# Starting the activations' sums twelve steps earlier, in tiles that begin 224 bytes off a multiple of 256

## The chip, the cores and the metric

The kernel runs on one core of one Trainium2 chip. The metric is the device time of one execution in microseconds (us), as the median of several runs. The engines are named as in the profile: PE (TensorE matmul), PEld (its weight loads), DVE (VectorE), ACT (ScalarE), POOL (GpSimd) and SP (SyncE).

## What is computed

The reference is a trunk of two layers on 256 tokens of width 2048, in float32. Layer 0 mixes with an mLSTM and a gated linear recurrence, layer 1 with dilated attention; each mixer ends in an output projection, and each layer ends in a SwiGLU feed-forward block with 5632 hidden columns. The part that matters here is the norm, the feed-forward block and what stands between them:

```python
x = x + mixer(rmsnorm(x, norm)) @ w_out        # the output projection
h = rmsnorm(x, f_norm[l])
x = x + (jax.nn.silu(h @ w1) * (h @ w3)) @ w2  # the feed-forward block
```

## The kernel before, in words

**Steps.** All weights stream through SBUF once. The kernel writes down a list of `steps`; a step is half of one weight tile: two k-blocks of 128 rows by 512 columns. `emit_step` (L340) runs one step: it splits the weights of the steps up to three ahead (`emit_split`, L213) into a high part on ACT (`wh`, L228) and a low part on DVE (`wl`, L229), issues the step's matmuls, and then calls `run_tasks` (L278) once. A float32 product is made of three matmuls: high by high, high by low, low by high. The activations are the stationary operand (PE loads 128x128 of them per matmul), the weights the moving one.

**Tasks.** Everything that isn't a weight product is a Python generator. `run_tasks` advances each urgent one, then up to three (`CONC`) of the queue, by one `yield`. So a task that yields n times is spread over n steps, and the engines' instructions stand in the order in which steps and tasks wrote them. A step may carry a function under `"before"`, which is called when the step begins, for instance to queue a task. Where a step needs something that a task hasn't made yet, `until` (L286) runs tasks until its flag is set.

**The output projection** (`out_proj`, L1184) has four groups of 512 columns and 32 steps; the last 16 are column groups 2 and 3, eight steps each. When a group ends, `norm_evac` (L407) adds it to the residual `xres` on DVE (L414), squares it on ACT (L417), has PE transpose it into PSUM (`nT`, L146) and writes the transposed, gain-scaled activations in two halves to `xT` (L440 on ACT, L441 on DVE). It then sets the flag of that quarter of `xT`.

**The feed-forward block** (`ffn`, L989) has 11 groups of 512 hidden columns. A group is 16 steps: `w1` and `w3` alternate, two steps each, over the four quarters of `xT`. After its `w3` part the group's result is transposed by PE (`hTp`, L146). After groups 0 to 2, 3 to 5, 6 to 8 and 9 to 10 come the steps of `w2`.

**Seven products.** In groups 1 to 10 the `w1` steps of quarters 1 to 3 (`SEVEN`) multiply a 2x2 block matrix with seven instead of eight block products (`seven_products`, L304): 21 matmuls of 256 columns instead of 12 of 512. For this they need sums of the weights' blocks (`weight_sums`, L197, made anew for each weight tile, `ws` and `wf`) and sums of the activations' blocks. The latter are made once per feed-forward block by the task `act_sums` (L1056) and kept in three tiles `sf`, one per quarter, each with two pairs of k-blocks. For each of the six pairs the task makes one sum over `xT` (L1067), four sums and differences (L1071, L1072, L1074, L1075, into `sb`), a high part on ACT (L1077) and a low part on DVE (L1079), with a `yield` behind each of the five stages. It waits for the flag of its quarter of `xT` first. `seven_products` takes four stationary operands of each pair from `sf`, in high and low: 12 of its 21 matmuls load from it.

**Where the sums begin.** The task is queued by the first step of the feed-forward block (L1117). Group 0 doesn't use its result; group 1 needs the first pair in its fifth step and the sixth pair in its fourteenth.

**Tiles.** `sf`, `hT` (the `w2` operand), the residual `xres` and others take slots of one pool with eight buffers (`slot`, L87), each of 2112 floats, that is 8448 bytes or 33 times 256. A tile begins where its slot begins, at a multiple of 256 bytes.

Of the kernel before, what the change touches and what calls it, by code (L numbers as in the profile page):

```python
# [9 lines left out]
F32 = mybir.dt.float32  # L10
F32R = mybir.dt.float32r
# [6 lines left out]
P = 128  # L18
# [50 lines left out]
def trunk_kernel(ctx: ExitStack, tc: tile.TileContext, a, out):  # L69
# [14 lines left out]
    mxp = ctx.enter_context(tc.tile_pool(name="mxp", bufs=2, space=PSUM))  # L84
    ctx.enter_context(tc.manual_schedule())

    def slot(shape, dt=F32, name="s8"):  # L87
        t = s8p.tile([P, SLOT], dt, tag="s8", name=name)
        n = int(np.prod(shape))
        v = t[:, :n]  # L90
        if len(shape) == 1:
            return v
        pat = {2: "p (a b) -> p a b", 3: "p (a b c) -> p a b c", 4: "p (a b c d) -> p a b c d"}[len(shape)]
        return v.rearrange(pat, **dict(zip("abcd"[1:], shape[1:])))
# [6 lines left out]
    def ev(name="ev"):  # L101
        return evp.tile([P, CW], F32, tag="ev", name=name)
# [50 lines left out]
    steps = []  # L153
    x_in = {}

    def load_xT(k0, n):

        i, r = divmod(k0, 8)
        if i not in x_in:
            x_in[i] = slot((8, S), name="xin")  # L160
        SP.dma_start(x_in[i][:, r:r + n, :], a["xT"][:, k0:k0 + n, :])
# [77 lines left out]
    def add_unit(src, ch, kb0, first, last, act, seven=None):  # L239

        items.append(wload(src, len(items)))
        it = len(items) - 1
        for h in range(2):
            steps.append({
                "item": it, "half": h, "last_half": h == 1, "ch": ch, "kb": kb0 + 2 * h, "act": act,
                "first": first and h == 0, "last": last and h == 1, "wide": False, "before": None, "seven": seven,
            })
# [21 lines left out]
    urgent, queue, active = [], [], []  # L269
# [201 lines left out]
    def rg_block(b):  # L471
        def gen(ch):
            if b == 0:
                rg["xc"] = slot((RB, S), name="xc")
            xc = rg["xc"][:, b, :]
            e = ev("xr")
            xp = e[:, :260]
            V.memset(e[:, 0:2], 0.0)
            V.memset(e[:, 258:260], 0.0)
            while "rstd_e" not in flags:  # L480
                yield
            join(ch.acc[0], e[:, 2:258])
            ch.acc = None
            V.tensor_tensor(e[:, 2:258], e[:, 2:258], cur["rB"], op=ALU.mult)
            yield
            w = cpk[:, C_W + 4 * b:C_W + 4 * b + 4]
            A.activation(
                xc, xp[:, 2:258], AF.Identity, bias=cpk[:, C_B + b:C_B + b + 1], scale=w[:, 2:3],
            )
            for j in (0, 1, 3):  # L490
                V.scalar_tensor_tensor(xc, xp[:, j:j + S], w[:, j:j + 1], xc, op0=ALU.mult, op1=ALU.add)
            if b == RB - 1:
                queue.append(rg_scans())
            yield

        return gen

    def rg_scans():
        while "gates" not in flags:
            yield  # L500
        rg["h"] = slot((RB, S), name="rgh")
        wts = [rg_weights(0)]
        for c in range(RB // 2):
            if c + 1 < RB // 2:
                wts.append(rg_weights(c + 1))
            yield from rg_scan(c, wts.pop(0))
# [482 lines left out]
    def ffn(l, gains, nxt):  # L989
# [64 lines left out]
        sf = {}  # L1054

        def act_sums():  # L1056

            for g in SEVEN:
                while f"xT{gains}_{g}" not in flags:
                    yield  # L1060
                two = slot((2, 4, 2, P), F32R, "sf")
                for j, kb in enumerate((4 * g, 4 * g + 2)):
                    f = two[:, j]
                    v = ev("sa")
                    x = xT[:, kb:kb + 2].bitcast(F32)
                    vv = v.rearrange("p (j t) -> p j t", j=2)
                    V.tensor_tensor(vv, x[:, :, 0, :], x[:, :, 1, :], op=ALU.add)  # L1067
                    a11, a21, a12, a22 = (vv[:, j, t * P:(t + 1) * P] for j in range(2) for t in range(2))
                    w = ev("sb").rearrange("p (k t) -> p k t", k=4)
                    yield  # L1070
                    V.tensor_tensor(w[:, 0], a21, a22, op=ALU.add)  # L1071
                    V.tensor_tensor(w[:, 2], a11, a21, op=ALU.subtract)  # L1072
                    yield
                    V.tensor_tensor(w[:, 1], w[:, 0], a11, op=ALU.subtract)  # L1074
                    V.tensor_tensor(w[:, 3], a12, w[:, 1], op=ALU.subtract)  # L1075
                    yield
                    A.copy(f[:, :, 0, :], w)  # L1077
                    yield
                    V.tensor_tensor(f[:, :, 1, :], w, f[:, :, 0, :].bitcast(F32), op=ALU.subtract)  # L1079
                    sf[kb] = f  # L1080
                    flags.add(f"sf{l}_{kb}")
                    yield
# [5 lines left out]
        at_first = len(steps)  # L1088
        for hidx, (c0, c1) in enumerate(UPS):
# [23 lines left out]
            for n, kgs in ((0, range(c0, c1 - 1)), (1, range(c0, c1 - 1)), (0, (c1 - 1,)), (1, (c1 - 1,)),  # L1113
                           (2, range(c0, c1)), (3, range(c0, c1))):
                for kg in kgs:
                    add_unit(a["w2"][l, n][kg], chs[n], 4 * kg, kg == c0, kg == c1 - 1, act_h)
        steps[at_first]["before"] = lambda: queue.append(act_sums())  # L1117
        return ssq


# [78 lines left out]
    steps[first + 8]["before"] = load_x  # L1199

    ffn(0, G_F0, G_O)

    act = act_norm(G_O)
# [3 lines left out]
    out_proj(a["w_o"], G_F1, act_o, "ssq_o1", ((0, 1, 2), (3,)))  # L1207

    ssq = ffn(1, G_F1, -1)

    def load_fg():
# [25 lines left out]
    n = NCD - 1  # L1237
# [104 lines left out]
```

## Time and profile before

| what | value |
|---|---|
| median of 3 runs | 2220.28 us (2219.53 to 2221.06) |
| the profiled execution: its time | 2219.59 us |
| the profiled execution: its span | 2217.8 us |
| mean granted TensorE clock | 0.996 |
| PE busy | 2195.3 us, 11492 matmuls |
| DVE busy | 1588.9 us |
| ACT busy | 1156.3 us |
| DMA | 417.53 MB, mean 188 GB/s |

The span is what the trace covers, from the first to the last instruction; the 1.8 us between it and the execution's own time lie around it. Busy time on PE counts from a matmul's start to its modelled end, and matmuls overlap, so the distance between the starts of two matmuls says more about PE's pace than their durations. In the list of waits an arrow names the instruction that ended a wait; in the timeline the same stands in brackets, with the idle time ahead of the instruction. The granted clock is the share of TensorE's full clock that it was allowed in a stretch.

### The profile page before, as it was taken

How to read it: one execution, taken by the hardware profiler on the slowest of the kernel's cores; microseconds unless marked ns; L12 is line 12 of the kernel's file. 1: busy time of each engine (PE TensorE's matmuls, PEld its weight loads, DVE VectorE, ACT ScalarE, POOL GpSimd, SP SyncE). 2: the span in 40 equal slices, each digit the busy share in tenths (PEclk: the TensorE clock that was granted, in tenths of full speed). 3: DMA queues.
4: the chain of work that ended last, by engine and by line, in shares of the span. 5: the costliest groups of instructions: out<-in, count | busy, mean ns of one | idle time of the engine just before them, and what ended most of it. 6: DMA issues, size and time to landing. Idle time of an engine off the chain costs nothing.

```text
span 2217.8 us, 28894 instructions
## 1 busy us (share of the span) xinstructions
PE 2195.3 (99%) x11492; PEld 1881.5 (85%) x11492; DVE 1588.9 (72%) x2160; ACT 1156.3 (52%) x1555; POOL 22.6 (1%) x37
## 2 busy tenths in 40 slices
PE   9999999999999999999999999999999999999998
PEld 7887888888888888888888888888888888888886
DVE  6877756875787688578666676567867885886686
ACT  6666555544455455445554555455544553554454
POOL 0000000000000000000000000000000000000000
PEclk9999999999999999999999999999999999999999
DMA  7444555555555555555554555455555655555653
GB/s 280 174 143 148 193 201 199 171 190 190 199 181 207 179 201 201 194 197 191 177 191 174 180 185 175 171 182 180 189 190 190 208 190 190 183 203 197 215 192 131
DMA packets 61471, 417.53 MB, mean 188 GB/s; under 512 B 7060, under 2 KB 7956, under 8 KB 12568
## 3 DMA queue, kind: packets, MB, share of 16 engines
q1 hardware_dynamic: 58616, 406.69, 52.9%
q0 software_dynamic: 2288, 8.39, 1.1%
q8 instruction: 90, 1.47, 0.2%
q10 hardware_dynamic: 432, 0.61, 0.1%
q14 instruction: 45, 0.37, 0.0%
HBM read 413.56 MB, written 2.10 MB: 187 GB/s over the span
## 4 chain that ended last, share of the span: by engine, by line
PE 90%; DVE 6%; ACT 2%; issue 1%; DMA 0%; SPq 0%; POOL 0%; POOLq 0%; DVEq 0%; ACTq 0%
PE acc L300 20%; PE acc L301 20%; PE acc L302 20%; PE acc L361 9%; PE acc L362 5%; PE ext L338 2%; PE ext L337 2%; PE ext L336 2%; DVE wl L229 2%; PE acc L338 2%; PE acc L336 2%; PE acc L337 2%; ACT wh L228 1%; PE hTp L146 1%; PE rgp L524 1%
## 5 line engine op out<-in xcount | busy, mean ns | idle before, releaser
L229 DVE TENSOR_TENSOR wl<-raw,wh 128x1024 fp32r<-128x1024 f32 (+1 forms) x770 | 928.7, 1220 | 519.9 <-ACT wh L228 517.1
L228 ACT CAST wh<-raw 128x1024 fp32r<-128x1024 f32 (+1 forms) x770 | 794.0, 1046 | 518.8 <-PE acc L302 376.2
L300 PE MATMUL acc<-wh,xT 128*128 128x512 f32 x1184 | 467.5, 395 | 0.0
L301 PE MATMUL acc<-wl,xT 128*128 128x512 f32 x1184 | 462.9, 391 | 1.0 <-DVE wl L229 1.0
L302 PE MATMUL acc<-wh,xT 128*128 128x512 f32 x1184 | 461.6, 390 | 0.0
L361 PE MATMUL acc<-xT,wh 128*128 128x512 f32 x896 | 321.7, 402 | 0.5 <-ACT v L731 0.5
L300 PE MATMUL acc<-wh,hT 128*128 128x512 f32 x704 | 276.1, 392 | 0.0
L302 PE MATMUL acc<-wh,hT 128*128 128x512 f32 x704 | 274.3, 390 | 0.0
L301 PE MATMUL acc<-wl,hT 128*128 128x512 f32 x704 | 274.1, 389 | 0.1
L302 PEld LDWEIGHTS acc<-wh,xT 128*128 128x128 f32 x1184 | 222.7, 188 | 47.2
L300 PEld LDWEIGHTS acc<-wh,xT 128*128 128x128 f32 x1184 | 223.4, 189 | 45.7 <-issue 1.5
L301 PEld LDWEIGHTS acc<-wl,xT 128*128 128x128 f32 x1184 | 223.1, 188 | 44.9 <-DVE wl L229 2.3
L362 PE MATMUL acc<-xT,wl 128*128 128x256 f32 x896 | 251.2, 280 | 0.2 <-DVE wl L229 0.2
L209 ACT CAST wf<-ws 128x512 fp32r<-128x512 f32 x180 | 111.9, 622 | 201.1 <-DVE ws L202 152.5
L361 PEld LDWEIGHTS acc<-xT,wh 128*128 128x128 f32 x896 | 168.3, 188 | 39.5 <-ACT v L731 0.6
L362 PEld LDWEIGHTS acc<-xT,wl 128*128 128x128 f32 x896 | 169.2, 189 | 1.1 <-DVE wl L229 0.5
L302 PEld LDWEIGHTS acc<-wh,hT 128*128 128x128 f32 x704 | 132.1, 188 | 27.8
L301 PEld LDWEIGHTS acc<-wl,hT 128*128 128x128 f32 x704 | 132.3, 188 | 27.4 <-DVE wl L229 0.5
L300 PEld LDWEIGHTS acc<-wh,hT 128*128 128x128 f32 x704 | 132.2, 188 | 26.8
L210 DVE TENSOR_TENSOR wf<-ws,wf 128x512 fp32r<-128x512 f32 x180 | 113.3, 684 | 0.0
L338 PE MATMUL ext<-wf,sf 128*128 128x256 f32 x240 | 68.7, 286 | 4.6 <-DVE sf L1079 4.6
L336 PE MATMUL ext<-wf,sf 128*128 128x256 f32 x240 | 68.3, 285 | 3.6 <-ACT sf L1077 3.6
(278 smaller groups left out, 2731.8 us busy)
## 6 DMA issues: line engine op xcount, KB each, us to landing
raw<-in_w SPq DMA_DIRECT2D x264, 1024.0 KB, 4.9
raw<-in_w_aqk SPq DMA_DIRECT2D x32, 1024.0 KB, 4.9
raw<-in_w_out SPq DMA_DIRECT2D x16, 1024.0 KB, 4.9
raw<-in_w_av SPq DMA_DIRECT2D x16, 1024.0 KB, 4.9
raw<-in_w_o SPq DMA_DIRECT2D x16, 1024.0 KB, 4.9
raw<-in_w_xr SPq DMA_DIRECT2D x8, 1024.0 KB, 6.8
raw<-in_w_qk SPq DMA_DIRECT2D x8, 1024.0 KB, 4.9
raw<-in_w_og SPq DMA_DIRECT2D x8, 1024.0 KB, 4.8
```

The costliest lines, as they stand in the source:

```text
L209: A.copy(f[:, 0], t)
L210: V.tensor_tensor(f[:, 1], t, f[:, 0].bitcast(F32), op=ALU.subtract)
L228: A.copy(hi[:, k], raw[:, k])
L229: V.tensor_tensor(lo[:, k], raw[:, k], hi[:, k].bitcast(F32), op=ALU.subtract)
L300: PE.matmul(acc, xh, hi[:, j, :], start=f, stop=False)
L301: PE.matmul(acc, xh, lo[:, j, :], start=False, stop=False)
L302: PE.matmul(acc, xl, hi[:, j, :], start=False, stop=e)
L336: PE.matmul(o, xh, wh, start=new, stop=False)
L337: PE.matmul(o, xh, wl, start=False, stop=False)
L338: PE.matmul(o, xl, wh, start=False, stop=end)
L361: PE.matmul(acc, wh[:, j, :], x2.rearrange("p a b -> p (a b)"), start=f, stop=False)
L362: PE.matmul(acc[:, :S], wl[:, j, :], x2[:, 0, :], start=False, stop=e)
```

## The change

Two things change. The task `act_sums` is queued by the step that lies twelve before the feed-forward block's first, in the fifth of the eight steps of the output projection's column group 2. And `slot` gets an argument `off`, with which the `sf` tiles begin 56 floats, 224 bytes, behind the start of their slot (they have 2048 floats, so they still fit).

```diff
-    def slot(shape, dt=F32, name="s8"):
+    def slot(shape, dt=F32, name="s8", off=0):
         t = s8p.tile([P, SLOT], dt, tag="s8", name=name)
         n = int(np.prod(shape))
-        v = t[:, :n]
+        v = t[:, off:off + n]
...
-                two = slot((2, 4, 2, P), F32R, "sf")
+                two = slot((2, 4, 2, P), F32R, "sf", off=56)
...
-        steps[at_first]["before"] = lambda: queue.append(act_sums())
+        steps[at_first - 12]["before"] = lambda: queue.append(act_sums())
```

The number of instructions is the same on every engine, and the order of PE's is the same too. On DVE and ACT the task's instructions move. Each step of weights has one L229, so L229 rows count steps. First DVE's rows at the end of the output projection of layer 0, in the kernel before: from the residual addition of column group 2 (L414) on.

```order
L229 TENSOR_TENSOR wl<-raw,wh 128x1024 x6
L414 TENSOR_TENSOR xres<-acc,xres 128x512 x2
L229 TENSOR_TENSOR wl<-raw,wh 128x1024
L441 SCALAR_TENSOR_TENSOR xT<-nT,cpk,xT 128x256 x2
L229 TENSOR_TENSOR wl<-raw,wh 128x1024
L441 SCALAR_TENSOR_TENSOR xT<-nT,cpk,xT 128x256 x2
L229 TENSOR_TENSOR wl<-raw,wh 128x1024 x5
L414 TENSOR_TENSOR xres<-acc,xres 128x512 x2
L229 TENSOR_TENSOR wl<-raw,wh 128x1024
L441 SCALAR_TENSOR_TENSOR xT<-nT,cpk,xT 128x256 x4
```

The same place in the changed kernel, around the residual addition of column group 3:

```order
L1079 TENSOR_TENSOR sf<-sb,sf 128x4x128
L229 TENSOR_TENSOR wl<-raw,wh 128x1024
L1067 TENSOR_TENSOR sa<-xT 128x512
L229 TENSOR_TENSOR wl<-raw,wh 128x1024
L1071 TENSOR_TENSOR sb<-sa 128x128
L1072 TENSOR_TENSOR sb<-sa 128x128
L414 TENSOR_TENSOR xres<-acc,xres 128x512 x2
L229 TENSOR_TENSOR wl<-raw,wh 128x1024
L441 SCALAR_TENSOR_TENSOR xT<-nT,cpk,xT 128x256 x4
```

The sums of the third pair stand there, with two small additions ahead of L414. At column group 2 the low part of the first pair (L1079) stands behind L414, not ahead of it.

Then DVE's rows in group 1 of the feed-forward block of layer 0, before, at the sixth pair's last instruction; `wf` and `ws` belong to the sums of the weights, L1004 to the group's evacuation:

```order
L1067 TENSOR_TENSOR sa<-xT 128x512
L229 TENSOR_TENSOR wl<-raw,wh 128x1024
L1071 TENSOR_TENSOR sb<-sa 128x128
L1072 TENSOR_TENSOR sb<-sa 128x128
L229 TENSOR_TENSOR wl<-raw,wh 128x1024
L1074 TENSOR_TENSOR sb<-sb,sa 128x128
L1075 TENSOR_TENSOR sb<-sa,sb 128x128
L229 TENSOR_TENSOR wl<-raw,wh 128x1024 x2
L1079 TENSOR_TENSOR sf<-sb,sf 128x4x128
L229 TENSOR_TENSOR wl<-raw,wh 128x1024
L1004 TENSOR_TENSOR u_3884<-ext,up 128x256
```

And the sixth pair's last instruction in the changed kernel:

```order
L210 TENSOR_TENSOR wf<-ws,wf 128x512 x3
L229 TENSOR_TENSOR wl<-raw,wh 128x1024
L1079 TENSOR_TENSOR sf<-sb,sf 128x4x128
L229 TENSOR_TENSOR wl<-raw,wh 128x1024
L1041 TENSOR_TENSOR hT<-hTp,hT 128x2x256
L229 TENSOR_TENSOR wl<-raw,wh 128x1024
L1041 TENSOR_TENSOR hT<-hTp,hT 128x2x256
L229 TENSOR_TENSOR wl<-raw,wh 128x1024
L202 TENSOR_TENSOR ws<-raw 128x512
```

Between this L1079 and the same L1004 there are now 13 instructions of L229, where there was one: it has moved twelve steps ahead. In the program's order, 168 matmuls now stand between the last pair's low part and the matmul that loads it, where none stood. Layer 1 moves in the same way.

## The prediction, on record before the changed kernel ran

> **What bounds the kernel now.** I read the page's shares of busy time and its chain first, to learn which engine's time is the program's time.
>
> ```profile
> PE 2195.3 (99%) x11492; PEld 1881.5 (85%) x11492; DVE 1588.9 (72%) x2160; ACT 1156.3 (52%) x1555; POOL 22.6 (1%) x37
> PE 90%; DVE 6%; ACT 2%; issue 1%; DMA 0%; SPq 0%; POOL 0%; POOLq 0%; DVEq 0%; ACTq 0%
> ```
>
> TensorE (PE) is busy for 99% and carries 90% of the chain. Time can change only where PE waits, where its clock is lowered, or where its instructions themselves last longer. So the next view is the list of waits, for PE alone (total us, times, longest).
>
> ```profile
> PE ext L338 <- DVE sf L1079: 4.6, 2, 2.3
> PE ext L336 <- ACT sf L1077: 3.6, 2, 1.8
> PE num L796 <- ACT q L763: 1.4, 1, 1.4
> PE nT L146 <- DVE xres L414: 1.1, 5, 0.3
> ```
>
> The two longest are both for `sf`, the sums tiles that the change moves: 4.6 + 3.6 = 8.2 us, once per feed-forward block each. The timeline of PE shows the first block's wait (start, us, engine, line, operation).
>
> ```profile
> 443.36 0.28 PE L337 MATMUL acc<-wf,xT 128*128 128x256 f32 x1
> 443.48 0.28 PE L338 MATMUL acc<-wf,xT 128*128 128x256 f32 x1
> 445.57 0.39 PE L336 MATMUL ext<-wf,sf 128*128 128x256 f32 x1 [1.80 <-ACT sf L1077]
> 448.38 0.58 PE L338 MATMUL ext<-wf,sf 128*128 128x256 f32 x1 [2.31 <-DVE sf L1079]
> 448.76 0.41 PE L336 MATMUL ext<-wh,xT 128*128 128x256 f32 x1
> 448.97 0.41 PE L337 MATMUL ext<-wl,xT 128*128 128x256 f32 x1
> ...
> 453.02 0.63 PE L301 MATMUL acc<-wl,xT 128*128 128x512 f32 x1
> 454.08 0.40 PE L301 MATMUL acc<-wl,xT 128*128 128x512 f32 x1
> ```
>
> The reader is to see two things. The high half of `sf` (ACT, L1077) comes 1.8 us late and its low half (DVE, L1079) another 2.3 us. And after it the matmuls start 0.21 us apart (448.76, 448.97) where they had started 0.12 apart (443.36, 443.48). The view by stretches says why: window, PE busy, then the granted clock.
>
> ```profile
> 440.00:447.00 7.00, 4.26 (x28) 1.00 0.41 150
> 447.00:453.80 6.80, 5.42 (x22) 0.50 0.46 154
> 454.00:461.00 7.00, 7.00 (x33) 1.00 0.44 150
> 1566.50:1573.30 6.80, 5.04 (x21) 0.50 0.51 171
> ```
>
> For some 6.8 us, from the second gap on, the granted clock is 0.50, in the second block as in the first, and then 1.00 again. So a wait costs its idle time and a slow stretch behind it. The Trainium skill ("TensorE: Matmul & The Clock Gate", section "Why this matters for your kernels") asks for no PE-idle gaps above about 3 us. Here two shorter gaps, 1.80 and 2.31 us with two matmuls between them, are followed by the lower clock, so the trace is stricter than that sentence.
>
> **The change part by part.** What both waits cost together I take from the timeline of PE at the transposes that end each column group's `up` work (L146 into `hTp`): groups 1 and 2 of the first block, then of the second.
>
> ```profile
> 416.28 0.60 PE L146 MATMUL hTp<-cst,up 128*128 128x128 f32 x4
> 466.79 0.60 PE L146 MATMUL hTp<-cst,up 128*128 128x128 f32 x4
> 510.07 0.60 PE L146 MATMUL hTp<-cst,up 128*128 128x128 f32 x4
> 1536.16 0.60 PE L146 MATMUL hTp<-cst,up 128*128 128x128 f32 x4
> 1586.51 0.60 PE L146 MATMUL hTp<-cst,up 128*128 128x128 f32 x4
> 1629.79 0.60 PE L146 MATMUL hTp<-cst,up 128*128 128x128 f32 x4
> ```
>
> Group 1 takes 466.79 − 416.28 = 50.51 us and group 2, with the same 16 steps and the same sums of weights, 510.07 − 466.79 = 43.28. The first block loses 7.23 us in group 1; the second 50.35 − 43.28 = 7.07. Together 14.30 us, of which 8.2 are the waits and 6.1 the half clock with the pipeline's refill.
>
> *The earlier start.* It adds and removes no instruction. Why the tile is late now stands in the timelines of DVE and ACT.
>
> ```profile
> 442.71 0.28 DVE L1071 TENSOR_TENSOR sb<-sa 128x128 f32<-128x128 f32 x1
> 444.57 0.29 DVE L1075 TENSOR_TENSOR sb<-sa,sb 128x128 f32<-128x128 f32 x1
> 446.50 1.23 DVE L229 TENSOR_TENSOR wl<-raw,wh 128x1024 fp32r<-128x1024 f32 x1 [0.50 <-ACT wh L228]
> 447.64 0.69 DVE L1079 TENSOR_TENSOR sf<-sb,sf 128x512 fp32r<-128x512 f32 x1
> 444.90 0.62 ACT L1077 CAST sf<-sb 128x512 fp32r<-128x512 f32 x1 [2.32 <-DVE sb L1075]
> ```
>
> The task yields five times per tile pair, so 30 steps for its six pairs, and the last pair is used in the 30th step of the block (16 steps of group 0, then the fourteenth of group 1). It has no slack, and its last two instructions are issued when PE stands already at the matmul. With twelve steps' lead, the first two pairs and half of the third are done beside the output projection. The last two pairs still need the projection's last block, but that is ready in the first step of the feed-forward block, before their turn comes. In DVE's order the last L1079 now stands thirteen steps' L229 ahead of group 1's L1004 instead of one, twelve steps of 43.28/16 = 2.7 us, some 32 us, against a lateness of 1.80 + 2.31 = 4.1. So the whole 14.30 goes, and what is late next is what group 2 shows: no wait. PE's order doesn't change at all.
>
> What hides the moved work is the idle time of DVE and ACT in the projection.
>
> ```profile
> 362.26 1.23 DVE L229 TENSOR_TENSOR wl<-raw,wh 128x1024 fp32r<-128x1024 f32 x1 [1.45 <-ACT wh L228]
> 363.41 1.28 DVE L414 TENSOR_TENSOR xres<-acc,xres 128x512 f32<-128x512 f32 x2
> 366.42 1.03 PE L146 MATMUL nT<-cst,xres 128*128 128x128 f32 x8
> ```
>
> A step there has one L229 of 1.23 us and 1.45 us of idle time, and a pair asks for at most one L1079 or the equally large L1067 (0.69) or two small ones (0.57) per step. The place to watch is L414, which PE's transposes into `nT` wait for: L1071 and L1072 now stand ahead of the last one, 0.57 us. It ends at 364.69 and the transposes start at 366.42, so 1.73 us of slack hide it. If that cover were gone, 0.57 us would fall on PE, twice: 1.1 us. ACT's L1077 (0.62) passes L417 and L228, which the splits' three steps of lead cover. The task issues no DMA, so SP's and POOL's queues pass nothing, and the slots that `sf` takes had their last reader 225 matmuls or more before. I take nothing for all of this. The bounds are 0 and 1.1 us: a gain is excluded, since PE waits for nothing else of DVE there.
>
> *The offset of 224 bytes.* Its writers are 12 instructions on ACT and 12 on DVE with slack. Its readers are PE's weight loads. These rows have the load of `sf` (min/median/max ns), the loads of two other tiles (busy us, then mean ns), and two starts of matmuls on the timeline.
>
> ```profile
> L336 PEld LDWEIGHTS acc<-wh,sf x120: 192/192/330, 421.6 to 2157.3; 128*128 128x128 f32 x120
> L302 PEld LDWEIGHTS acc<-wh,xT 128*128 128x128 f32 x1184 | 222.7, 188 | 47.2
> L302 PEld LDWEIGHTS acc<-wh,hT 128*128 128x128 f32 x704 | 132.1, 188 | 27.8
> 75.15 0.27 PE L362 MATMUL acc<-xT,wl 128*128 128x256 f32 x1
> 75.26 0.40 PE L361 MATMUL acc<-xT,wh 128*128 128x512 f32 x1
> ```
>
> Twelve of the 21 matmuls of a seven-product step load `sf`; with 10 groups of 6 such steps in 2 blocks that is 1440 loads. No weight load of this shape reads off a multiple of 256 in this trace, so the price is bounded, not read. Below: the load may be what sets the 0.12 us between these matmuls, since the same shape follows a longer one 0.11 us apart (75.15, 75.26); were `sf` loads to become that much quicker, say 7 ns, 1440 of them would give 10 us back. Above: 128 columns in 0.12 us are 0.94 ns each, and if the load went by aligned pieces of 64 bytes (16 columns), a row of 512 bytes that begins 32 bytes before a multiple of 64 would touch nine pieces instead of eight: 15 ns more, 1440 × 15 = 21.6 us. I take zero, by the nearest rows: slots are 8448 bytes, 33 × 256, so the `hT` tiles begin at odd and at even multiples of 256, and they load in the same 188 ns as `xT`; and 224 is itself a multiple of 32. The Trainium skill ("SBUF — State Buffer", section "Specifications (TRN2)") gives 16-byte cachelines in that memory; by it 224 is 14 whole lines, a row stays at 32 of them, and the price is zero too; no run here shows it yet.
>
> *The sum.* 14.30 − 0 − 0 = 14.3 us. The profiled execution took 2219.59 (span 2217.8), which gives 2205.3. The median of the runs is 2220.28, 0.7 above it, so the median forecast is 2220.28 − 14.3 = 2206.0.
>
> **The rivals.**
>
> *A: the forecast*, 2206, with 2 us to either side (the 1.1 us above, and the runs' own spread, 2219.53 to 2221.06). Chance 0.70.
>
> *B: the offset slows the loads*, the case on the other side. Place: the 1440 loads of `sf`. For it: the seven-product steps run at the load's pace, 0.12 us for 256 columns. Against it: equal 188 ns for two kinds of slots. It eats the gain from 14.3/1440 = 9.9 ns per load. At 15 ns the time is 2206.0 + 21.6 = 2227.6. Chance 0.15: 0.10 for 13 ns or more (slower by over 0.2%), 0.05 for about 10 (no change).
>
> *C: the offset quickens the loads*, by the 7 ns above: 2206.0 − 10 = 2196. Only the 0.11 us speaks for it. Chance 0.08.
>
> *D: only the waits go*, and the half clock has a cause of its own: 2220.3 − 8.2 = 2212. Against it: both stretches at 0.50 stand right at the two waits, and at 454 us the clock is 1.00 again. The skill's sentence on gaps over 3 us, cited above, would allow this case, as neither gap here is that long. Chance 0.04.
>
> *E: the change doesn't do what it says*: the last pairs still wait for the projection's last block and might be late again; then nothing changes, 2220. Against it: the twelve steps in DVE's order. Chance 0.03.
>
> **How the numbers follow.** Likeliest is A, 2206.0. The range from 2196 to 2214 holds A, C and D, 0.82; B and E (0.18) lie above it. A measurement of this kernel can tell 0.2%, 4.4 us, from no change. Faster by more than that: A, C, D, 0.82. Within it: E and B's middle, 0.08. Slower: 0.10.
>
> **What would show it.** Right: no wait of PE for `sf` in the list, group 1 as long as group 2 (43.3 us), the granted clock at 1.00 at about 447 and 1560 us, and 0.12 us between matmuls with `sf`. Wrong: starts of `sf` matmuls further apart (B) or closer (C), which the load rows and group 2's length would show (12 × 6 loads per group: 15 ns are 1.1 us); a half clock without a wait (D); a new wait of `nT` for L414 beyond 1.1 us, or of DVE's L229 in the projection; `sf` still in PE's list (E).

## The result and the profile after

| | before | after |
|---|---|---|
| median of 4 runs each, same chip | 2219.91 us (2218.67 to 2221.06) | 2200.86 us (2200.33 to 2201.15) |
| profiled execution | 2219.59 us, span 2217.8 | 2201.15 us, span 2199.1 |
| granted clock, mean | 0.996 | 0.999 |

The change is faster by 0.9%: ratio 0.9914 with a 95% interval of 0.9897 to 0.9931, or 19 us. The forecast of 2206.0 had the sign and the larger part. Some 5 us more went than it counted.

The busy shares and the chain of the page after:

```profile
PE 2184.5 (99%) x11492; PEld 1871.8 (85%) x11492; DVE 1588.8 (72%) x2160; ACT 1157.0 (53%) x1555; POOL 21.8 (1%) x37
PE 94%; DVE 3%; ACT 2%; issue 1%; DMA 0%; SPq 0%; POOL 0%; POOLq 0%; DVEq 0%; ACTq 0%
```

The number of instructions is the same on every engine. DVE's part of the chain fell from 6% to 3%. PE's busy time fell as well, 2195.3 to 2184.5: that can't come from a wait, since waits are not busy time. The half clock stretched the matmuls before, and something else has to be found for the rest.

The waits of PE after (total us, times, longest):

```profile
PE num L796 <- ACT q L763: 1.4, 1, 1.4
PE nT L146 <- DVE xres L414: 1.1, 5, 0.3
PE warm L1127 <- DVE ones L1121: 1.1, 1, 1.1
PE acc L301 <- DVE wl L229: 1.0, 2, 0.8
```

Both waits for `sf` are gone. The wait of `nT` for L414, where the moved work might have shown, has the same 1.1 us in 5 waits.

The stretches where the two gaps and the clock of 0.50 had been, in the second block some 9 us earlier than before (window and its length, then PE, PEld, DVE, ACT, POOL busy, granted clock, DMA share, GB/s):

```profile
440.00:447.00 7.00, 7.00 (x53) 6.63 (x52) 3.77 (x4) 3.03 (x3) 0.00 (x0) 1.00 0.72 241
447.00:453.80 6.80, 6.80 (x32) 5.62 (x31) 4.69 (x8) 3.48 (x6) 0.00 (x0) 1.00 0.61 214
1557.00:1564.00 7.00, 7.00 (x33) 5.78 (x32) 4.69 (x8) 3.68 (x6) 0.00 (x0) 1.00 0.61 221
1560.00:1567.00 7.00, 7.00 (x33) 5.79 (x32) 5.15 (x7) 3.23 (x4) 0.00 (x0) 1.00 0.37 139
```

PE is busy throughout and the clock is 1.00 in both blocks. The timeline of PE after, at the transposes that end the column groups, first block and second:

```profile
416.82 0.60 PE L146 MATMUL hTp<-cst,up 128*128 128x128 f32 x4
459.87 0.60 PE L146 MATMUL hTp<-cst,up 128*128 128x128 f32 x4
502.91 0.60 PE L146 MATMUL hTp<-cst,up 128*128 128x128 f32 x4
1527.02 0.60 PE L146 MATMUL hTp<-cst,up 128*128 128x128 f32 x4
1570.06 0.60 PE L146 MATMUL hTp<-cst,up 128*128 128x128 f32 x4
```

Group 1 is as long as group 2, 459.87 − 416.82 = 43.05 and 502.91 − 459.87 = 43.04 us, as the forecast wanted. But it wanted 43.28, the old length of group 2. Every group is 0.24 us shorter than the cleanest one before. The same shows in the stretch from one block's first such row to the other's. It was 1536.16 − 416.28 = 1119.88 us, of which 7.23 were group 1's loss; that leaves 1112.65. It is 1110.20 now: 2.45 us more went than the waits and the clock held, over ten groups.

DVE's timeline after, at the place in the projection that the prediction named:

```profile
363.96 0.28 DVE L1071 TENSOR_TENSOR sb<-sa 128x128 f32<-128x128 f32 x1
364.17 0.28 DVE L1072 TENSOR_TENSOR sb<-sa 128x128 f32<-128x128 f32 x1
364.37 1.28 DVE L414 TENSOR_TENSOR xres<-acc,xres 128x512 f32<-128x512 f32 x2
```

The two small additions stand ahead of L414 as foretold. L414 ends at 365.65 and PE's transposes start at 366.94, so 1.29 of the 1.73 us of slack are left.

### The profile page after: what moved, and what is told of

Its sections match the earlier page's. It is cut to its first block, busy times and chain, and to the rows that moved or that the text cites. A ratio compares the mean times of both kernels' runs of the same rounds, so it can differ in the third digit from the quotient of the medians.

```text
span 2199.1 us, 28884 instructions
## 1 busy us (share of the span) xinstructions
PE 2184.5 (99%) x11492; PEld 1871.8 (85%) x11492; DVE 1588.8 (72%) x2160; ACT 1157.0 (53%) x1555; POOL 21.8 (1%) x37
## 4 chain that ended last, share of the span: by engine, by line
PE 94%; DVE 3%; ACT 2%; issue 1%; DMA 0%; SPq 0%; POOL 0%; POOLq 0%; DVEq 0%; ACTq 0%
PE acc L300 21%; PE acc L301 21%; PE acc L302 21%; PE acc L361 9%; PE acc L362 5%; PE ext L338 3%; PE ext L337 3%; PE ext L336 3%; PE acc L337 2%; PE acc L336 2%; PE acc L338 2%; DVE wl L229 1%; ACT wh L228 1%; PE hTp L146 1%; PE rgp L524 1%
## 5 line engine op out<-in xcount | busy, mean ns | idle before, releaser
L229 DVE TENSOR_TENSOR wl<-raw,wh 128x1024 fp32r<-128x1024 f32 (+1 forms) x770 | 928.4, 1220 | 500.8 <-ACT wh L228 498.0
L361 PE MATMUL acc<-xT,wh 128*128 128x512 f32 x896 | 321.8, 402 | 0.5 <-ACT v L731 0.5
L302 PEld LDWEIGHTS acc<-wh,hT 128*128 128x128 f32 x704 | 132.2, 188 | 27.7
```

Source lines behind the costliest of these rows:

```text
L229: V.tensor_tensor(lo[:, k], raw[:, k], hi[:, k].bitcast(F32), op=ALU.subtract)
L302: PE.matmul(acc, xl, hi[:, j, :], start=False, stop=e)
L361: PE.matmul(acc, wh[:, j, :], x2.rearrange("p a b -> p (a b)"), start=f, stop=False)
```

## The experiments

The first two runs take the change apart. Most of the others weigh two theories for the missing 5 us. One looks at the loaded tile alone: PE loads a 128x128 tile faster when it begins off a multiple of 256 bytes. The other looks at the difference: what counts is whether the loaded tile and the streamed tile of one matmul begin at the same place modulo 256. Two such tiles are called in step below; in the kernel before, all tiles named here begin at a multiple of 256. Narrow steps are the ordinary ones, which load activations and stream 512 columns of weights; wide steps, in the mixers, load weights and stream `xT`. "Loaded" is the 128-column operand (`xT`, `hT`, `oT`, `ya`, `yb`, `sf`; in the wide steps `wh` and `wl`) and "streamed" the other (`wh`, `wl`, `wf`; in the wide steps `xT`). Each median stands beside runs of the kernel before on the same chip.

### The start alone

```
-                two = slot((2, 4, 2, P), F32R, "sf", off=56)
+                two = slot((2, 4, 2, P), F32R, "sf")
```

> The earlier start alone, tiles at multiples of 256. If the two parts add up as the traces suggest (waits and half clock gone, and the rest from the offset), 2219.9 - 14.3 = 2205.6 us, with the matmuls of the seven-product steps 120 ns apart in both blocks. Rival: the earlier start or the other turn of the slots brings all of it, then 2200.9 us and about 117.5 ns.

Measured: 2206.44 us (2206.32 to 2206.86, 5 runs) beside 2219.32; ratio 0.9941 [0.9928, 0.9953]; 12.9 us. PE's timeline, group ends of both blocks:

```profile
417.26 0.60 PE L146 MATMUL hTp<-cst,up 128*128 128x128 f32 x4
460.57 0.60 PE L146 MATMUL hTp<-cst,up 128*128 128x128 f32 x4
503.87 0.60 PE L146 MATMUL hTp<-cst,up 128*128 128x128 f32 x4
1529.95 0.60 PE L146 MATMUL hTp<-cst,up 128*128 128x128 f32 x4
1573.24 0.60 PE L146 MATMUL hTp<-cst,up 128*128 128x128 f32 x4
```

Groups 1 and 2 of the first block take 43.31 and 43.30 us, the length of group 2 before. From block to block it is 1112.69 us, against the 1112.65 that were left of before without its loss. So the moved work, which in the second layer lies inside this stretch, costs 0.04 us, and the step "I take nothing" holds. Group 1 gains 50.51 − 43.31 = 7.20 us in the first block, nearly the forecast's 7.23, and 50.35 − 43.29 = 7.06 in the second, for 7.07. Most of what the medians' 12.9 lacks of 14.3 lies ahead of the first row, which stands at 417.26 here and at 416.28 before. It stands at 417.03 where the start was not moved (next) and at 416.27 in a kernel where it was (`off=8`, below), so the move is not its cause.

### The offset alone

```
-        steps[at_first - 12]["before"] = lambda: queue.append(act_sums())
+        steps[at_first]["before"] = lambda: queue.append(act_sums())
```

> The offset alone, the task begins with the block as before. If the parts add up: the two waits and the half clock stay (group 1 some 7 us longer than group 2), and the 2520 matmuls of the seven-product steps start about 2 ns closer: 2219.9 - 4.7 = 2215.2 us. Rival, the offset does nothing: 2219.9 us and 120 ns.

Measured: 2214.43 us (2213.64 to 2215.8, 11 runs); ratio 0.9978 [0.9969, 0.9987]; 4.9 us. PE's waits, the group ends and the window in which the clock was 0.50 before:

```profile
PE ext L338 <- DVE sf L1079: 4.6, 2, 2.3
PE ext L336 <- ACT sf L1077: 3.6, 2, 1.8
```

```profile
417.03 0.60 PE L146 MATMUL hTp<-cst,up 128*128 128x128 f32 x4
466.64 0.60 PE L146 MATMUL hTp<-cst,up 128*128 128x128 f32 x4
509.69 0.60 PE L146 MATMUL hTp<-cst,up 128*128 128x128 f32 x4
```

```profile
447.00:453.80 6.80, 4.67 (x23) 4.55 (x24) 1.83 (x2) 1.17 (x3) 0.00 (x0) 0.75 0.55 196
```

The waits are those of before to the tenth, and group 1 still loses 49.61 − 43.05 = 6.56 us. That it isn't 7.23 goes with the clock: over this window the mean is 0.75, where it was 0.50 before. Cut into pieces of 0.4 us, the trace has the lower clock for some 3.4 us (449.3 to 452.8) behind the same two gaps that some 6.8 us followed before. So the same waits don't always cost the same slow stretch. Group 2 takes 43.05: the offset by itself gives the shorter groups. The two parts, 12.9 and 4.9, add up to 17.8 of the whole change's 19.05. What is left is of the size of the runs' own spread.

How this is spread over the instructions shows in the mean durations by line, of the matmuls and of the loads (busy us, then mean ns of one). With the start alone:

```profile
L338 PE MATMUL ext<-wf,sf 128*128 128x256 f32 x240 | 67.9, 283 | 0.0
L336 PEld LDWEIGHTS ext<-wf,sf 128*128 128x128 f32 x240 | 46.0, 192 | 0.0
```

And after:

```profile
L338 PE MATMUL ext<-wf,sf 128*128 128x256 f32 x240 | 67.3, 280 | 0.0
L336 PEld LDWEIGHTS ext<-wf,sf 128*128 128x128 f32 x240 | 45.4, 189 | 0.0
```

Both fall by 3 ns. By group length, 43.31 − 43.04 = 0.27 us over the 126 matmuls of six seven-product steps are 2.1 ns each on average, and 2520 such matmuls make 5.4 us, against 2206.44 − 2200.86 = 5.6 by medians. From start to start, the 1440 matmuls that load `sf` go from 119.9 to 116.7 ns on average, the 1080 that load `xT` only from 120.7 to 120.0.

### The streamed tiles shifted in place of sf

The loaded tiles stay at multiples of 256 and `wh`, `wl`, `wf` begin 224 bytes beyond; the pads are never read.

```
+    ctx.enter_context(tc.tile_pool(name="pad1", bufs=1)).tile([P, 56], F32, name="pad1")
     whp = ctx.enter_context(tc.tile_pool(name="whp", bufs=SPLIT_BUFS))
     wlp = ctx.enter_context(tc.tile_pool(name="wlp", bufs=SPLIT_BUFS))
+    ctx.enter_context(tc.tile_pool(name="pad2", bufs=1)).tile([P, 8], F32, name="pad2")
...
+    ctx.enter_context(tc.tile_pool(name="pad3", bufs=1)).tile([P, 56], F32, name="pad3")
     m4p = ctx.enter_context(tc.tile_pool(name="m4p", bufs=M4_BUFS))
+    ctx.enter_context(tc.tile_pool(name="pad4", bufs=1)).tile([P, 8], F32, name="pad4")
...
+                two = slot((2, 4, 2, P), F32R, "sf")
```

> The earlier start; the sums' tiles at multiples of 256, but the streamed tiles (wh, wl, wf) begin 224 bytes off. Theory 'difference': what counts is where the loaded tile begins as against the streamed one; then all 21 matmuls of a seven-product step gain, 117.5 ns or less, and about 2205.6 - 5 = 2200 us. Theory 'loaded tile': what counts is that the loaded tile itself is off; then 120 ns and 2205.6 us. The matmuls of 512 columns now stream from shifted tiles as well: no change is expected of them by either.

Measured: 2233.75 us (2233.39 to 2234.18, 5 runs); ratio 1.0064 [1.0051, 1.0076], slower than before, and 27.3 us behind the start alone. Mean durations by line of narrow and of wide steps, with the start alone and then here:

```profile
L300 PE MATMUL acc<-wh,hT 128*128 128x512 f32 x704 | 276.2, 392 | 0.0
L361 PE MATMUL acc<-xT,wh 128*128 128x512 f32 x896 | 322.2, 402 | 0.5 <-ACT v L731 0.5
```

```profile
L304 PE MATMUL acc<-wh,hT 128*128 128x512 f32 x704 | 280.4, 398 | 0.0
L365 PE MATMUL acc<-xT,wh 128*128 128x512 f32 x896 | 317.8, 396 | 0.5 <-ACT v L735 0.5
L342 PE MATMUL ext<-wf,sf 128*128 128x256 f32 x240 | 67.6, 282 | 0.0
```

Both theories missed: they expected no change of the 512-column matmuls. The loaded tiles of the narrow steps are where they always were, and yet their matmuls last 6 ns longer, and their starts lie 233 instead of 227 ns apart (medians). The loaded-tile theory has no place for that. In the wide steps, where `wh` is the loaded one, the shift takes 6 ns away. The groups agree: 464.89 − 421.13 = 43.76 us against 43.31, and from start to start its 120 narrow matmuls take 28.07 instead of 27.43 us (5.3 ns more each), its 126 others 15.00 instead of 15.17 (1.4 ns less each). Summed so over the kernel, the 6432 narrow matmuls take 35.6 us more, the seven-product ones 3.7 and the wide steps 4.2 us less: 27.7, against 27.3 by medians.

### Both shifted

As the last one, with `sf` at 224 too, so that `sf` and the streamed tiles are in step again.

```
-                two = slot((2, 4, 2, P), F32R, "sf")
+                two = slot((2, 4, 2, P), F32R, "sf", off=56)
```

> The earlier start; the sums' tiles and the streamed tiles both begin 224 bytes off. Theory 'difference': the sums' loads are in step with the streamed tiles again, so their 12 of 21 matmuls lose the gain, and the 9 with xT have it: between 2200.9 and 2205.6 us. Theory 'loaded tile': the sums' tiles are off as in the changed kernel, 117.5 ns and 2200.9 us.

Measured: 2234.85 us (2233.87 to 2235.12, 5 runs); ratio 1.0068 [1.0055, 1.0081]. One group:

```profile
420.17 0.60 PE L150 MATMUL hTp<-cst,up 128*128 128x128 f32 x4
463.98 0.60 PE L150 MATMUL hTp<-cst,up 128*128 128x128 f32 x4
```

43.81 us against 43.76 with `sf` at a multiple of 256. The same offset that shortened a group by 0.27 us lengthens it a little here, where it puts `sf` in step with what is streamed. By itself, 0.05 us a group is little to judge by. The starts tell more: the next matmul starts a median of 120 ns after one that loads `sf`, as with the start alone, and 117 ns after one that loads `xT`. With `sf` at a multiple of 256 (the last run) both are 117. So `sf` has lost its gain and `xT`, still out of step, has kept it, as the difference asks for. The time expected was 2200.9 to 2205.6; the narrow matmuls, at 398 ns again, took it out of that range.

### All loaded tiles of narrow and seven-product steps shifted

```
+    const.tile([P, 56], F32, name="pad1")
     xT = const.tile([P, KB, 2, S], F32R, name="xT")
+    const.tile([P, 8], F32, name="pad2")
...
-        yt = slot((4, 2, S), F32R, name="ya")
+        yt = slot((4, 2, S), F32R, name="ya", off=56)
```

`yb`, `oT` and `hT` get the same offset, `sf` keeps it; the streamed tiles stay.

> The changed kernel with every other large tile that PE loads in narrow and seven-product steps (xT, hT, oT, ya, yb) 224 bytes off as well; the streamed tiles stay. Theory 'difference': loaded 224 ahead of streamed is the good side (it took 512-column matmuls of the wide steps from 235 to 229 ns when their loaded tile was shifted), so the 6300 narrow matmuls fall below 227 ns, by 2 to 10 ns, and the seven-product steps' loads of xT join those of sf: 2201 - 13 to 2201 - 63, some 2170 us; the wide steps, where xT is streamed, now have the other sign and lose some us. Theory 'loaded tile' for the sums alone: 227 ns stays in narrow steps, the seven-product steps reach about 117 ns throughout, 2199 us.

Measured: 2233.78 us (2233.37 to 2234.12, 5 runs) beside 2219.14; ratio 1.0067 [1.0054, 1.0079]. Mean durations by line:

```profile
L302 PE MATMUL acc<-wh,hT 128*128 128x512 f32 x704 | 279.9, 398 | 0.0
L338 PE MATMUL ext<-wf,sf 128*128 128x256 f32 x240 | 67.0, 279 | 0.0
L363 PE MATMUL acc<-xT,wh 128*128 128x512 f32 x896 | 322.1, 401 | 0.4 <-ACT v L733 0.4
```

Both forecasts, some 2170 and 2199, missed. The narrow matmuls last 398 ns here too, so for them it doesn't matter which side is moved; shifting the loaded side does not quicken them, it costs as much as shifting the streamed side. The seven-product steps gain most here, as all their loads are out of step now: a group takes 465.90 − 422.33 = 43.57 us, 0.26 above the start alone; from start to start its narrow matmuls take 0.64 us more and its 126 others 0.38 less, 3.0 ns each. The wide steps, whose streamed tile is the shifted one, gain almost nothing (401). There the side does matter, which the difference alone doesn't say.

### Everything shifted

All pads and offsets of the last three together: every loaded and every streamed tile at 224.

```
+    ctx.enter_context(tc.tile_pool(name="pad1", bufs=1)).tile([P, 56], F32, name="pad1")
     whp = ctx.enter_context(tc.tile_pool(name="whp", bufs=SPLIT_BUFS))
...
+    const.tile([P, 56], F32, name="pad5")
     xT = const.tile([P, KB, 2, S], F32R, name="xT")
...
+                h = st["h", c] = slot((4, 2, S), F32R, name="hT", off=56)
```

> The earlier start, and all that PE loads or streams in the three large kinds of steps begins 224 bytes off a multiple of 256: xT, hT, oT, ya, yb, sf, wh, wl, wf. Theory 'difference': loaded and streamed tiles are in step again, so every kind of step is as with no offset: narrow 227 ns, seven-product 120, and 2206.4 us, as with the earlier start alone. Theory 'own start': narrow steps lose as soon as either tile is off, 233 ns, and the sums' loads gain, about 2230 us.

Measured: 2204.53 us (2203.93 to 2204.79, 5 runs) beside 2218.98; ratio 0.9934 [0.992, 0.9947]. Mean durations by line:

```profile
L306 PE MATMUL acc<-wh,hT 128*128 128x512 f32 x704 | 276.1, 392 | 0.0
L342 PE MATMUL ext<-wf,sf 128*128 128x256 f32 x240 | 67.8, 283 | 0.0
L367 PE MATMUL acc<-xT,wh 128*128 128x512 f32 x896 | 320.5, 400 | 0.5 <-ACT v L737 0.5
```

Narrow and seven-product matmuls are back at the durations of the start alone, 392 and 283, though none of these tiles begins at a multiple of 256. It is the difference that counts for both, not where one tile begins. The wide steps are not quite back: they are in step again, too, but at 400 ns, not 402. The 2 ns of the wide row make 322.2 − 320.5 = 1.7 of the 1.9 us that this kernel is under the start alone.

### Other offsets

The one number in the call, `off=4`, `8` and `32` elements, in three kernels:

```
-                two = slot((2, 4, 2, P), F32R, "sf", off=56)
+                two = slot((2, 4, 2, P), F32R, "sf", off=4)
```

> The changed kernel with 16 bytes instead of 224. Theory 'difference' with no say on size: any start out of step gives about the 117 to 118 ns that 32, 128 and 224 bytes gave, 2201 to 2202.5 us. Rival: the collision is between pieces of 32 bytes or more, then 16 bytes are still in step, 120 ns and 2206.4 us.

> The changed kernel with 32 bytes instead of 224. Theory 'difference' with its sign (streamed tiles 224 ahead gave 118.3 ns, which is loaded tiles 32 ahead modulo 256): 118.3 ns for the sums' matmuls, some 2203 us. If the distance alone counts, 224 and 32 are mirror images: 117.4 ns and 2201 us. If any start off a multiple of 256 will do: the same.

> The changed kernel with 128 bytes instead of 224. If the pattern repeats every 64 or 128 bytes, 128 is like 0: 120 ns and 2206.4 us. If it is 256 bytes long and the distance counts, 128 is the farthest: 117 ns or less, at most 2201 us.

Measured, beside 2200.86 at 224 bytes:

| offset | median (range), 5 runs each | ratio to before | groups 1, 2 |
|---|---|---|---|
| 16 bytes | 2201.97 (2201.48 to 2202.36) | 0.9922 [0.991, 0.9934] | 43.12, 43.12 |
| 32 bytes | 2201.75 (2201.73 to 2201.97) | 0.9923 [0.991, 0.9935] | 43.11, 43.11 |
| 128 bytes | 2202.45 (2202.31 to 2202.59) | 0.9926 [0.9913, 0.9938] | 43.14, 43.14 |

Any of them takes most of the 5 us; 224 is some 0.07 us a group better. Sixteen bytes are enough to be out of step. At 128 bytes the gain is there too, so the pattern does not repeat every 128 bytes or less; but the farthest place from a multiple of 256 is not the best, as one expectation had it.

### One step's lead

Without offset, the task begins one step ahead in place of twelve.

```
-        steps[at_first - 12]["before"] = lambda: queue.append(act_sums())
+        steps[at_first - 1]["before"] = lambda: queue.append(act_sums())
```

> Tiles at multiples of 256, the task one step ahead of its block instead of twelve. The high half of the last pair is in time then, the low half still 1 to 2 us late: one gap per block. If it takes the two gaps to lower the clock: it stays at 1.00, and the loss is the two gaps alone, 2206.4 + 2 to 4 = 2209 to 2210 us. If any wait of this size lowers it, 3 us more per block: 2215. If one step suffices for both halves: 2206.4.

Measured: 2212.73 us (2212.45 to 2216.02, 8 runs); ratio 0.9974 [0.9963, 0.9984]; 6.3 us behind the twelve steps. The timeline of PE at the one wait that is left, and the clock behind it:

```profile
445.02 0.39 PE L336 MATMUL ext<-wf,sf 128*128 128x256 f32 x1
445.25 0.28 PE L337 MATMUL ext<-wf,sf 128*128 128x256 f32 x1
447.83 0.39 PE L338 MATMUL ext<-wf,sf 128*128 128x256 f32 x1 [2.31 <-DVE sf L1079]
448.06 0.28 PE L336 MATMUL ext<-wh,xT 128*128 128x256 f32 x1
448.18 0.28 PE L337 MATMUL ext<-wl,xT 128*128 128x256 f32 x1
```

```profile
447.00:453.80 6.80, 5.97 (x35) 5.36 (x36) 4.42 (x8) 1.53 (x2) 0.00 (x0) 1.00 0.71 228
```

The high half is in time, the low half still 2.31 us late. With this gap alone, in both blocks, the clock stays 1.00 and the matmuls behind it start 0.12 us apart; before, with 1.80 us of gap two matmuls earlier, it fell to 0.50. Group 1 takes 463.84 − 417.06 = 46.78 us, 3.47 above the start alone: 2.31 of wait and 1.16 of refill and smaller waits around it (the list of waits has 0.7 us in two waits for `wl`, L229, that the start alone doesn't have). Twice 3.47 is 6.9, near the 6.3 measured and above the two waits' 4.6.

### Out of step in the wide steps, and `wf` out of step with `xT`

The changed kernel, with two additions: in the wide steps alone `wh` and `wl` begin 224 bytes further (one tile for both, of 33 × 256 bytes), and `wf` begins 128 beyond a multiple of 256. To make room, `rbp` has one buffer.

```
+        both = whp.tile([P, 4 * CW + 64], F32R, tag="wh", name="wh")
+        o = 56 if st["wide"] else 0
+        hi, lo = (both[:, o + 1024 * i:o + 1024 * (i + 1)].rearrange("p (a b) -> p a b", a=2) for i in range(2))
```

> The changed kernel with two more offsets, where the runs so far show a gain: in the wide steps the loaded weights begin 224 bytes off (their pair of matmuls took 352 ns in step and 347 out of step), and wf begins 128 bytes off, so that xT is out of step with it too. Theory 'difference': 896 pairs x 5 ns = 4.7 us, and 360 matmuls x 2.5 ns = 0.9 us less than the changed kernel, 2195 us. Rival: the wide steps' gain belonged to the shifted tiles of the run before in another way, then 2200 us.

Measured: 2196.52 us (2196.25 to 2197.13, 4 runs) beside 2218.98; ratio 0.9898 [0.9884, 0.9912]; 4.3 us under the changed kernel, and the fastest here. Its wide row by line:

```profile
L363 PE MATMUL acc<-xT,wh 128*128 128x512 f32 x896 | 317.9, 396 | 0.6 <-ACT v L733 0.6
```

The wide steps give 321.8 − 317.9 = 3.9 us of the 4.7 expected (321.8 is this row's busy time after). The groups take 43.04 as after, so `wf`'s place gives nothing that shows, where 0.9 us was expected.

## Why the prediction was right, and where it was short

**The waits and the clock, 14.30 us: right.** Waits gone, clock 1.00 at both places, group 1 equal to group 2. By group lengths the start alone gives 7.2 us in the first block and 7.1 in the second; by medians 12.9 us. How much of it is the half clock is not fixed: 6.8 us of it followed the gaps before, 3.4 with the offset alone.

**The moved work, 0: right.** The stretch from block to block, less group 1's loss, is the same to 0.04 us, and PE's wait for L414 still 1.1 us. The bound of 1.1 was not needed.

**The offset, "I take zero, by the nearest rows": mis-sized.** It measured −4.9 us alone and −5.6 on top of the earlier start, inside the bounds of −10 and +21.6. The measured 2200.86 lies below A's own 2204 to 2208; the range of 2196 to 2214 holds it only because it was drawn down to C. The step that failed is the choice of the nearest rows. The loads of `xT`, and of `hT` at odd and even multiples of 256, were all in step with the streamed tiles beside them, so their equal 188 ns said nothing of a tile that is out of step. The row behind the lower bound was the better guide: 0.12 us between matmuls of 256 columns and 0.11 where the shape followed a longer one; that both have one cause is not shown. And those 188 ns came from narrow steps, where the load is not the pace; the loads of `sf` in the page's own row stood at 192. After, that kind of load stands at 189.

The Trainium skill's cachelines of 16 bytes ("SBUF — State Buffer", section "Specifications (TRN2)") made the price zero as well, since 224 is 14 whole lines. Offsets of 16, 32, 128 and 224 bytes, all whole lines, changed the time, so that rule does not give the price here.

**B, the offset slows the loads (2227.6): wrong for this change**, whose loads fell by 3 ns. A cost of an offset does exist elsewhere: in narrow steps, 512-column matmuls out of step last 6 ns longer, and the three kernels that made them so took 2233.8 to 2234.9, beyond B's time. Their loads stay at 188 ns, so it isn't B's slower load. The change escapes this cost because only seven-product steps load `sf`.

**C, the offset quickens the loads (2196): right in direction**, with half its price: 119.9 − 116.7 = 3.2 ns for each load of `sf`, not 7, and 0.7 ns for each of `xT` between them. What it did not have is that the streamed tile's place counts as much.

**D, only the waits go (2212): refuted.** The clock is 1.00 without them, after and with the start alone. The prediction called the trace stricter than the 3 us of the Trainium skill ("TensorE: Matmul & The Clock Gate", section "Why this matters for your kernels"). The one step's lead qualifies that: a single gap of 2.31 us left the clock alone, in agreement with the Trainium skill's sentence; the pair of 1.80 and 2.31 us did not. That the chip takes the pair for one idle stretch is argued, not shown.

**E, nothing changes (2220): refuted**, `sf` is not in PE's list of waits.

## What to carry to other kernels

Look for the wait that ends last and start its producer early enough for all of the lateness: one step's lead removed one gap of two, twelve removed both. Where matmuls of 256 columns follow each other with a weight load each, try letting the loaded tile and the streamed tile begin at different places modulo 256 bytes; where a matmul streams 512 columns, first measure a few of them, since here being out of step cost 6 ns each in one kind of step and saved 6 in another, when the loaded side was moved. A row "nearest" to an unknown cost is near only if it differs in the one thing that is being changed.

## What the runs showed of the hardware

In this kernel a matmul's pace depends on where its two operands begin relative to each other, modulo 256 bytes: 128 bytes apart differs from 0, while the `hT` tiles at odd and at even multiples of 256 load and run alike. The 256-column matmuls of the seven-product steps, some 120 ns apart in step, are on average 1.3 to 3.2 ns faster out of step, whichever side is moved. The 512-column ones of the narrow steps go from 392 to 398 ns, whichever side is moved, and are back at 392 when both are; from start to start that is 227 and 233 to 234. The 512-column ones of the wide steps go from 402 to 396 when the loaded side is moved, only to 401 when the streamed side is, and to 400 when both are.

Two gaps of 1.80 and 2.31 us with two matmuls between them were followed by a granted clock of 0.50, for 6.8 us in one trace and 3.4 in another; a single gap of 2.31 us, in both blocks of one trace, was not.

What collides inside is open: no run here separates the load's reads from the stream's, and the wide steps' dependence on the side isn't explained by the difference alone. That 224 bytes are 1 us better than 16, 32 and 128 is also unexplained.
